# One more channel tile of a depthwise convolution moved from TensorE to ScalarE and GpSimd, in a hybrid decoder trunk

## The chip, the cores and the metric

The kernel runs on one core of a Trainium2 chip. A core has a matrix engine (TensorE, in the profile PE, with its weight loads as PEld), a vector engine (VectorE, DVE), a scalar engine (ScalarE, ACT), GpSimd (POOL) and a queue that issues DMAs (SyncE, SP). Each engine works through its own list of instructions in order, and semaphores tie the lists together. The metric is the device time of one launch in microseconds (us); lower is better.

## The reference

A trunk of two layers over 512 positions of 1024 channels, in float32. Layer 0 mixes tokens by a gated delta rule, layer 1 by a Conformer convolution module; each layer then attends to a memory of 256 positions and ends in an MLP. Only the Conformer module is touched:

```python
def conformer_conv(h, w_pw1, b_pw1, w_dw, b_dw, ln_g, ln_b, w_pw2, b_pw2):
    u = h @ w_pw1 + b_pw1
    u = u[..., :D_MODEL] * jax.nn.sigmoid(u[..., D_MODEL:])
    c = causal_depthwise_conv(u, w_dw) + b_dw
    c = jax.nn.silu(layer_norm(c, ln_g, ln_b))
    return c @ w_pw2 + b_pw2

# and in the trunk, for layer 1:
h = h + conformer_conv(rms_norm(h, cv_norm[j]), ...)
```

`causal_depthwise_conv` has a width of 31: each channel is convolved with its own 31 weights along the positions. The layer norm runs over the 1024 channels of a position.

## The kernel before

**Matrix products.** All of them run in float32 by splitting: a value is a high part (a cast, ACT) and a low part (value minus high part, DVE or POOL), and `mm3` (L227) multiplies high by high, high by low and low by high. Weights come in halves of 128x1024 from memory into `raw` (3 buffers); `wsplit` (L199) casts a half into `wh` (ACT, L207) and subtracts into `wl` (DVE or, for the halves of `pw1` and for every other half of K and V in layer 1, POOL; L70). `wh` and `wl` have 3 buffers each (`NW`), so the cast for half n waits until PE has done with half n-3.

**The Conformer stage** (`conformer`, L999) works on activations that lie channel by channel: 8 tiles m of 128 channels by 512 positions. The positions are kept in four phases (position modulo 4), so that a shift by d positions is a shift by d // 4 columns and a change of phase. `CONV_SEQ` (L1372) sets the order of PE's units: 16 units `("p", i)`, the two halves (value and gate) of the first pointwise product for each m, 24 products each; then 16 units `("k", i)`, the K and V products of the cross-attention that follows, which need nothing of the convolution and are there as work to lay beside it. `CONV_AFTER` (L1373) hangs other steps behind units. At the end of a tile's second half `pw_ev` (L1012) evicts both (`sg`, `pa` times the norm's `rb`, DVE), takes the sigmoid (ACT) and multiplies (DVE).

**The convolution has two forms.** For m = 0 to 3 (`NDVE` = 4) `dve_conv` (L1038) does it by taps: `x7` holds the four phases and the three shifted ones; the first tap is an ACT product into a PSUM tile `ca`, the 30 others are one DVE instruction each, `ca = x * w + ca` (L73); at the end ACT copies `ca` out (L1051). `turn` (L1059) then turns the tile back to positions by four PE transposes (`cvT`), adds it to the bias that lies in `Y` (DVE) and takes the statistics for the layer norm (`bn_stats`, DVE). For m = 4 to 7 `conv` (L1069) does it on PE: 16 small DMAs regroup the tile into `xg` (L1032), nine DMAs bring weights (`taps`, L991), and 72 products (64 of 128x128, L1078; 8 of 128x64, L1081) write `cv` already turned; DVE adds it to the bias in `Y` and takes statistics. `Y` (`cy`) is eight tiles, four of positions by two halves of channels, filled at the start with the bias by eight DMAs (L1006).

**The end of the stage.** `ln` (L1091) joins the statistics, takes the square root (ACT) and scales the eight `Y` tiles (DVE, L79). `ln_out` (L1106) turns a channel tile back (`lnT`, PE), applies silu (ACT, `la`) and splits the result (`lsh` ACT, `lsl` DVE). The second pointwise product, eight tiles of 24 PE products (`pw<-lsh`), needs all eight; its first result is evicted at `h<-pw`.

**Order.** The tile framework reorders instructions within each engine by its own priorities and writes out fixed lists; a tile whose buffer is taken waits for its release. What stands in an engine's list behind a waiting instruction waits with it.

Of the kernel before, what the change touches and what calls it, by code (L numbers as in the profile page):

```python
# [8 lines left out]
F32 = mybir.dt.float32  # L9
F32R = mybir.dt.float32r  # L10
AF = mybir.ActivationFunctionType
# [3 lines left out]
P = 128  # L15
NT = 512
NDVE = 4
KT = 8
# [3 lines left out]
_VECS = ["dn_norm", "cv_norm", "xa_norm0", "xa_norm1", "xa_mem0", "xa_mem1", "mlp_norm0", "mlp_norm1",  # L22
         "ln_g", "ln_b", "b_pw2"]
OFF = {n: 8 * i for i, n in enumerate(_VECS)}
# [5 lines left out]
OFF["w_tap"] = _o  # L30
_o += NDVE * 31
OFF["out_norm"] = _o
# [6 lines left out]
def tile_trunk(ctx, tc, xT, memT, prm_d, adt_d, bdw_d, tap_d, fin_d, w_ab, w_kq, w_v, w_z, w_dno, w_pw1, w_pw2,  # L39
# [951 lines left out]
    def taps(m):  # L991

        TAPS[m] = []
        for i in range(9):
            t = slot(s="tap")
            nc.sync.dma_start(out=t, in_=tap_d[m - NDVE, i])
            TAPS[m].append(t)

    def conformer(norm, hres, nxt):  # L999
# [4 lines left out]
        for y in Y:  # L1004
            for i in range(2):
                nc.sync.dma_start(out=y[i], in_=bdw_d[i * 512:(i + 1) * 512].partition_broadcast(P))  # L1006

# [4 lines left out]
        def pw_ev(m):  # L1012
# [4 lines left out]
            tt(dve, a, st.pop((m, 0)), norm.rb, ALU.mult)  # L1017
            if m < NDVE:
                x7 = fsp.tile([P, 1024], F32, tag="fs", name=nm("x7"))[:, 0:1008].rearrange("p (q t) -> p q t", q=7)
                pool.memset(x7[:, :, 0:10], 0.0)  # L1020
                stt(x7[:, 3:7, 8:136], c4(a), pc("b_pw1", m), c4(sg), ALU.add, ALU.mult)
                act.copy(x7[:, 0:3, 9:137], x7[:, 4:7, 8:136])
                todo.extend(dve_conv(m, x7))
                return
# [10 lines left out]

        todo, acc = [], {}

        def dve_conv(m, x7):  # L1038

            def tap(d):  # L1040
                w, u, e = pc("w_tap", m * 31 + 30 - d), d // 4, d % 4
                src = x7[:, 3 - e:7 - e, 8 - u:136 - u]
                if d == 0:
                    st["ca"] = psum("ca")
                    act.activation(c4(st["ca"]), src, AF.Copy, scale=w)  # L1045
                    return
                a = c4(st["ca"])
                stt(a, src, w, a, ALU.mult, ALU.add)
                if d == 30:
                    acc[m] = slot(s="ca")  # L1050
                    act.copy(acc[m], st.pop("ca"))  # L1051

            return [lambda d=d: tap(d) for d in range(31)]

        def taps_dve(us):
# [3 lines left out]
        def turn(m):  # L1059
# [4 lines left out]
            for r in range(4):  # L1064
                y = Y[r][m // 4][:, m % 4 * P:m % 4 * P + P]
                tt(dve, y, ps[:, r * P:(r + 1) * P], y, ALU.add)
                dve.bn_stats(out=bn[:, (r * 8 + m) * 6:(r * 8 + m) * 6 + 6], in_=y)
# [50 lines left out]
        for i, (kind, u) in enumerate(CONV_SEQ):  # L1118
            if kind == "p":
                m, hf = divmod(u, 2)  # L1120
                pw_mm(m, hf)
                if (m, hf) == (0, 0):
                    norm.stat()
                if (m, hf) == (1, 0):
                    norm.spread()
                    pw_ev(0)
                if hf == 1 and m > 0:
                    pw_ev(m)
            else:
# [179 lines left out]
    def finish(hid, cur):  # L1309
# [3 lines left out]
        for c, g in LAST:  # L1313
# [14 lines left out]
            if g == 0:  # L1328
# [69 lines left out]
def _taps(np, w):  # L1398
# [11 lines left out]
    e = np.concatenate([e[:, :, :, 0:8].reshape(128, 8, 128), e[:, :, :, 8].reshape(128, 8, 16)], axis=2)  # L1410
    e = e.reshape(4, 32, 8, 9, 16)[:, :, NDVE:]
    t = np.zeros((8 - NDVE, 9, 4, 32, 16, 32), w.dtype)
    for c in range(32):
        t[:, :, :, c, :, c] = e[:, c].transpose(1, 2, 0, 3)
    return t.reshape(8 - NDVE, 9, 128, 512)


def _layout(np, i):
# [3 lines left out]
    def vec(v):  # L1422
# [6 lines left out]
            i["xa_mem_norm"][1], i["mlp_norm"][0], i["mlp_norm"][1], i["cv_ln_g"][0],  # L1429
            i["cv_ln_b"][0], i["cv_b_pw2"][0], i["cv_b_pw1"][0]]  # L1430
    cols = [vec(v) for v in vecs]
    cols.append(i["dn_w_conv"][0].T.reshape(24, 128, 4).transpose(1, 0, 2).reshape(128, 96))
    cols.append(i["cv_w_dw"][0].T.reshape(8, 128, 31)[:NDVE].transpose(1, 0, 2).reshape(128, NDVE * 31))
    cols.append(i["dn_out_norm"][0].reshape(128, 1))
# [39 lines left out]
```

## Time and profile before

| What | Value |
|---|---|
| median of 3 runs | 1562.23 us (1561.81 to 1562.45) |
| the profiled execution | 1561.98 us, span 1560.3 us |
| mean granted TensorE clock | 0.991 |
| busy share of the span | PE 98%, DVE 58%, ACT 42%, POOL 12% |
| the Conformer's first product starts | 863.2 us into the span |
| its second pointwise product starts | 1041.2 us |
| first two results of that product evicted | 1047.90 and 1052.43 us |

All times of rows are from the start of the span. The profile shows a busy time, a start and what ended the idle time before an instruction; a group joins instructions of one line, engine and operation. PE's products overlap in the array, so the duration of one (0.39 us for 128x512) is longer than the step from one to the next (0.23 us), which counts for sums. DVE's instructions overlap a little too. A long product list such as `L229`/`L230`/`L231` is `mm3`.

### The profile page before, as it was taken

The numbers are of one execution on the slowest core, as the hardware profiler recorded it, in microseconds if no ns is written. First come the engines' busy times: TensorE is split into PE (matmuls) and PEld (weight loads), VectorE is DVE, ScalarE is ACT, GpSimd is POOL, SyncE is SP. The second block draws the span as 40 slices with busy tenths as digits, with TensorE's granted clock in tenths as the row PEclk, the third lists the DMA queues.
The fourth block names the chain that finished last, engine by engine and source line by source line (L and its number), as shares of the span: only waits on it lengthen the run. The fifth ranks groups of instructions, "written<-read, shape, count | busy, mean of one in ns | idle before, by whom it ended". The sixth has DMA issues, their size and how long they took to land.

```text
span 1560.3 us, 19403 instructions
## 1 busy us (share of the span) xinstructions
PE 1527.7 (98%) x7628; PEld 1285.7 (82%) x7628; DVE 901.2 (58%) x1373; ACT 655.0 (42%) x1018; POOL 187.0 (12%) x202
## 2 busy tenths in 40 slices
PE   9999996999999999999999999999999999999998
PEld 7888885988888888888888889978888888888886
DVE  6798887767555444343435499864545443444441
ACT  6847654554444433232314331264444432323332
POOL 1311212001112000000002441212112000000000
PEclk9999997999999999999999999999999999999999
DMA  5122121352212232222334625443203223332231
GB/s 181 55 87 68 63 78 46 107 189 69 91 58 78 88 101 99 95 95 95 99 100 155 200 87 166 161 141 95 80 29 108 95 96 100 101 96 95 95 108 54
DMA packets 51115, 156.17 MB, mean 100 GB/s; under 512 B 6608, under 2 KB 8912, under 8 KB 51024
## 3 DMA queue, kind: packets, MB, share of 16 engines
q1 hardware_dynamic: 51024, 154.93, 30.4%
q8 instruction: 60, 0.98, 0.3%
q14 instruction: 31, 0.25, 0.1%
HBM read 151.76 MB, written 2.10 MB: 99 GB/s over the span
## 4 chain that ended last, share of the span: by engine, by line
PE 90%; DVE 5%; issue 2%; ACT 1%; DMA 1%; SPq 1%; POOL 0%; DVEq 0%; POOLq 0%; ACTq 0%
PE up L229 7%; PE up L230 7%; PE up L231 7%; PE dn L229 7%; PE dn L231 7%; PE dn L230 7%; PE pw L229 3%; PE pw L231 3%; PE pw L230 3%; PE h L230 2%; PE h L229 2%; PE h L231 2%; PE q L229 2%; PE xo L230 2%; PE q L231 2%
## 5 line engine op out<-in xcount | busy, mean ns | idle before, releaser
L207 ACT CAST wh<-raw 128x1024 fp32r<-128x1024 f32 x248 | 260.4, 1051 | 673.9 <-PE dn L230 190.4
L70 DVE TENSOR_TENSOR wl<-raw,wh 128x1024 fp32r<-128x1024 f32 x224 | 275.6, 1231 | 97.3 <-ACT wh L207 95.9
L229 PE MATMUL up<-xh,wh 128*128 128x512 f32 x512 | 200.2, 391 | 0.0
L231 PE MATMUL up<-xh,wl 128*128 128x512 f32 x512 | 199.2, 389 | 0.0
L230 PE MATMUL up<-xl,wh 128*128 128x512 f32 x512 | 199.2, 389 | 0.0
L231 PE MATMUL dn<-uh,wl 128*128 128x512 f32 x448 | 174.3, 389 | 0.0
L229 PE MATMUL dn<-uh,wh 128*128 128x512 f32 x448 | 174.3, 389 | 0.0
L230 PE MATMUL dn<-ul,wh 128*128 128x512 f32 x448 | 174.3, 389 | 0.0
L70 DVE TENSOR_TENSOR h<-dn,h 128x512 f32<-128x512 f32 x56 | 41.8, 747 | 163.3 <-PE dn L231 163.3
L73 DVE SCALAR_TENSOR_TENSOR rl<-up,rb 128x512 f32<-128x512 f32 x64 | 44.2, 691 | 156.9 <-PE up L231 156.9
L229 PEld LDWEIGHTS up<-xh,wh 128*128 128x128 f32 x512 | 96.1, 188 | 20.3 <-issue 0.5
L231 PEld LDWEIGHTS up<-xh,wl 128*128 128x128 f32 x512 | 96.1, 188 | 20.2
L230 PEld LDWEIGHTS up<-xl,wh 128*128 128x128 f32 x512 | 96.1, 188 | 20.1 <-issue 0.5
L70 POOL TENSOR_TENSOR sq<-sq,sq 128x512 f32<-128x512 f32 x30 | 48.7, 1623 | 460.5 <-ACT sq L304 460.5
L231 PEld LDWEIGHTS dn<-uh,wl 128*128 128x128 f32 x448 | 84.1, 188 | 17.6
L230 PEld LDWEIGHTS dn<-ul,wh 128*128 128x128 f32 x448 | 84.1, 188 | 17.4
L229 PEld LDWEIGHTS dn<-uh,wh 128*128 128x128 f32 x448 | 84.1, 188 | 17.3
L73 DVE SCALAR_TENSOR_TENSOR ca<-x,prm,ca 128x512 f32<-128x512 f32 x120 | 88.0, 750 | 3.0 <-ACT ca L1045 1.2
L229 PE MATMUL h<-xh,wh 128*128 128x512 f32 x192 | 79.7, 415 | 1.7 <-ACT xh L297 1.7
L230 PE MATMUL h<-xl,wh 128*128 128x512 f32 x192 | 77.7, 405 | 0.6 <-DVE xl L73 0.6
L231 PE MATMUL h<-xh,wl 128*128 128x512 f32 x192 | 77.2, 402 | 0.0
L70 POOL TENSOR_TENSOR wl<-raw,wh 128x1024 fp32r<-128x1024 f32 x24 | 57.5, 2402 | 114.4 <-ACT wh L207 93.8
(336 smaller groups left out, 3024.6 us busy)
## 6 DMA issues: line engine op xcount, KB each, us to landing
raw<-w_up SPq DMA_DIRECT2D x64, 512.0 KB, 3.6
raw<-w_dn SPq DMA_DIRECT2D x64, 512.0 KB, 3.6
raw<-w_pw SPq DMA_DIRECT2D x24, 512.0 KB, 3.7
tap<-tap SPq DMA_DIRECT2D x36, 256.0 KB, 5.5
raw<-w_kq SPq DMA_DIRECT2D x16, 512.0 KB, 3.7
raw<-w_k SPq DMA_DIRECT2D x16, 512.0 KB, 3.8
raw<-w_vv SPq DMA_DIRECT2D x16, 512.0 KB, 4.2
raw<-w_q SPq DMA_DIRECT2D x16, 512.0 KB, 3.6
```

Of the source, the lines that this page charges most:

```text
L70: return e.tensor_tensor(out=o, in0=a, in1=b, op=op)
L73: dve.scalar_tensor_tensor(out=o, in0=a, scalar=s, in1=b, op0=op0, op1=op1)
L207: ins = [act.copy(h, raw)]
L229: pe.matmul(ps, wh, xh, start=first, stop=False)
L230: pe.matmul(ps, wh, xl, start=False, stop=False)
L231: pe.matmul(ps, wl, xh, start=False, stop=last)
```

## The change

It has six parts.

1. `NDVE` becomes `NTAP` = 5: the tiles m = 0 to 4 go by taps, m = 5 to 7 by PE. The weights for PE shrink to three tiles, and `pw_ev` and `taps` follow.
2. Tile m = 0 has a new form, `pool_conv`. Its input is laid into `xp` (four phases, no shifted copies). Tap 0 is an ACT product; each of the 30 others is an ACT product into a new tile `cvp` (one instruction where the shift keeps the phase, else two) and one POOL addition into `ca`. They are dealt out by `taps_pool`: two behind each `p` unit, one behind each `k` unit, three behind each `c` step. Tiles 1 to 4 take the DVE form.
3. The bias enters with the first tap (ACT, `AF.Identity` with a bias), and `turn` no longer adds: ACT copies each of the four transposed pieces to `Y`, and DVE takes the statistics from PSUM. Four of the eight bias DMAs fall away.
4. `CONV_AFTER` is new: the turns stand at their tiles' ends, the turn of tile 4 and the layer norm stand behind unit 27, and the eight `ln_out` behind units 29 to 31 (before: layer norm behind unit 23, `ln_out` behind units 26 to 31).
5. The norm's `spread` and the first `pw_ev` come one unit earlier.
6. The diagonal of that norm (`dg`) is made on DVE rather than POOL.

```diff
-NDVE = 4
+NTAP = 5
...
         for y in Y:
-            for i in range(2):
-                nc.sync.dma_start(out=y[i], in_=bdw_d[i * 512:(i + 1) * 512].partition_broadcast(P))
+            nc.sync.dma_start(out=y[1], in_=bdw_d[512:1024].partition_broadcast(P))
...
-            if m < NDVE:
+            if m == 0:
+                x4 = c4(wp.tile([P, 544], F32, tag="cv", name=nm("xp"), bufs=NCV))
+                pool.memset(x4[:, :, 0:8], 0.0)
+                stt(x4[:, :, 8:136], c4(a), pc("b_pw1", m), c4(sg), ALU.add, ALU.mult)
+                todo_p.extend(pool_conv(m, x4))
+                return
+            if m < NTAP:
...
+        def pool_conv(m, x4):
+            a = acc[m] = slot(s="ca")
+
+            def tap(d):
+                w, u, e = pc("w_tap", m * 31 + 30 - d), d // 4, d % 4
+                if d == 0:
+                    act.activation(c4(a), x4[:, :, 8:136], AF.Identity, scale=w, bias=pc("b_dw", m))
+                    return
+                b = slot(s="cvp")
+                act.activation(c4(b)[:, e:4], x4[:, 0:4 - e, 8 - u:136 - u], AF.Copy, scale=w)
+                if e:
+                    act.activation(c4(b)[:, 0:e], x4[:, 4 - e:4, 7 - u:135 - u], AF.Copy, scale=w)
+                tt(pool, a, a, b, ALU.add)
...
-                    act.activation(c4(st["ca"]), src, AF.Copy, scale=w)
+                    act.activation(c4(st["ca"]), src, AF.Identity, scale=w, bias=pc("b_dw", m))
...
+        def taps_pool(n):
+            for _ in range(min(len(todo_p), n)):
+                todo_p.pop(0)()
...
-                y = Y[r][m // 4][:, m % 4 * P:m % 4 * P + P]
-                tt(dve, y, ps[:, r * P:(r + 1) * P], y, ALU.add)
+                y = ps[:, r * P:(r + 1) * P]
+                act.copy(Y[r][m // 4][:, m % 4 * P:m % 4 * P + P], y)
                 dve.bn_stats(out=bn[:, (r * 8 + m) * 6:(r * 8 + m) * 6 + 6], in_=y)
...
-                if (m, hf) == (1, 0):
+                if (m, hf) == (0, 1):
                     norm.spread()
-                    pw_ev(0)
-                if hf == 1 and m > 0:
+                if hf == 1:
                     pw_ev(m)
             else:
                 kv_unit(1, u)
             taps_dve(5.4 if kind == "p" else 2.8)
+            taps_pool(2 if kind == "p" else 1)
             for what, m, *js in after.pop(i, ()):
...
+                taps_pool(3 if what == "c" else 0)
...
-    n3 = Norm("cv_norm", deng=pool)
-    h = mlp(0, n2, h, n3, lambda: (mem_gain(1, 0), mem_gain(1, 1), taps(NDVE)))
+    n3 = Norm("cv_norm")
+    h = mlp(0, n2, h, n3, lambda: (mem_gain(1, 0), mem_gain(1, 1), taps(NTAP)))
...
-CONV_AFTER = [(3, ("t", 5)), (11, ("d", 0)), (12, ("c", 4, 0, 1)), (13, ("c", 4, 2, 3)), (13, ("t", 6)),
-              (14, ("c", 5, 0, 1, 2, 3)), (14, ("t", 7)), (15, ("d", 1)), (16, ("c", 6, 0, 1, 2, 3)), (18, ("d", 2)),
-              (18, ("c", 7, 0, 1, 2, 3)), (23, ("d", 3)), (23, ("l", 0))]
-CONV_AFTER += [(_i, ("o", _m)) for _m, _i in enumerate((26, 27, 28, 29, 30, 30, 31, 31))]
+CONV_AFTER = [(3, ("t", 6)), (11, ("d", 1)), (13, ("c", 5, 0, 1, 2, 3)), (13, ("t", 7)), (15, ("c", 6, 0, 1, 2, 3)),
+              (16, ("d", 2)), (17, ("c", 7, 0, 1, 2, 3)), (19, ("d", 0)), (23, ("d", 3)), (27, ("d", 4)), (27, ("l", 0))]
+CONV_AFTER += [(_i, ("o", _m)) for _m, _i in enumerate((29, 29, 30, 30, 30, 31, 31, 31))]
```

The rest of the diff packs the weights and biases for the new split. In the instruction lists of the changed kernel, the four statistics and the four copies of a turn alternate strictly, each waiting for the other engine's last one.

More of the change, by code (lines that the diff above doesn't have):

```diff
@@ L22 @@
 _VECS = ["dn_norm", "cv_norm", "xa_norm0", "xa_norm1", "xa_mem0", "xa_mem1", "mlp_norm0", "mlp_norm1",
-         "ln_g", "ln_b", "b_pw2"]
+         "ln_g", "ln_b", "b_pw2", "b_dw"]
 OFF = {n: 8 * i for i, n in enumerate(_VECS)}
@@ L30 @@
 OFF["w_tap"] = _o
-_o += NDVE * 31
+_o += NTAP * 31
 OFF["out_norm"] = _o
@@ L995, in taps @@
             t = slot(s="tap")
-            nc.sync.dma_start(out=t, in_=tap_d[m - NDVE, i])
+            nc.sync.dma_start(out=t, in_=tap_d[m - NTAP, i])
             TAPS[m].append(t)
@@ L1034, in pw_ev @@
             xg[m] = x4
-        todo, acc = [], {}
+        todo, todo_p, acc = [], [], {}
+        def pool_conv(m, x4):
[10 more added lines that the diff above has]
+                tt(pool, a, a, b, ALU.add)
+            return [lambda d=d: tap(d) for d in range(31)]
         def dve_conv(m, x7):
@@ L1410, in _taps @@
     e = np.concatenate([e[:, :, :, 0:8].reshape(128, 8, 128), e[:, :, :, 8].reshape(128, 8, 16)], axis=2)
-    e = e.reshape(4, 32, 8, 9, 16)[:, :, NDVE:]
-    t = np.zeros((8 - NDVE, 9, 4, 32, 16, 32), w.dtype)
+    e = e.reshape(4, 32, 8, 9, 16)[:, :, NTAP:]
+    t = np.zeros((8 - NTAP, 9, 4, 32, 16, 32), w.dtype)
     for c in range(32):
         t[:, :, :, c, :, c] = e[:, c].transpose(1, 2, 0, 3)
-    return t.reshape(8 - NDVE, 9, 128, 512)
+    return t.reshape(8 - NTAP, 9, 128, 512)
 def _layout(np, i):
@@ L1429, in _layout @@
             i["xa_mem_norm"][1], i["mlp_norm"][0], i["mlp_norm"][1], i["cv_ln_g"][0],
-            i["cv_ln_b"][0], i["cv_b_pw2"][0], i["cv_b_pw1"][0]]
+            i["cv_ln_b"][0], i["cv_b_pw2"][0], i["cv_b_dw"][0], i["cv_b_pw1"][0]]
     cols = [vec(v) for v in vecs]
     cols.append(i["dn_w_conv"][0].T.reshape(24, 128, 4).transpose(1, 0, 2).reshape(128, 96))
-    cols.append(i["cv_w_dw"][0].T.reshape(8, 128, 31)[:NDVE].transpose(1, 0, 2).reshape(128, NDVE * 31))
+    cols.append(i["cv_w_dw"][0].T.reshape(8, 128, 31)[:NTAP].transpose(1, 0, 2).reshape(128, NTAP * 31))
     cols.append(i["dn_out_norm"][0].reshape(128, 1))
```

## The prediction

> **What bounds it now.** I read the page first, then the stage's stretches, the chain of waits, and the instructions of DVE and POOL in order of time.
>
> ```profile
> PE 1527.7 (98%) x7628; PEld 1285.7 (82%) x7628; DVE 901.2 (58%) x1373; ACT 655.0 (42%) x1018; POOL 187.0 (12%) x202
> ```
> ```profile
> 900.00:920.00 20.00, 20.00 (x90) 16.57 (x89) 19.58 (x29) 7.18 (x10) 8.39 (x5) 1.00 0.32 105
> ...
> 1020.00:1040.00 20.00, 17.85 (x82) 14.34 (x83) 13.06 (x18) 14.13 (x19) 3.07 (x2) 0.91 0.44 141
> ```
>
> PE is the bound overall: only work taken off PE, or a wait of PE, moves the end. The stretches (columns: length, then busy time of PE, PEld, DVE, ACT, POOL, then clock) show that in the Conformer DVE is as full as PE (19.6 of 20 us), while ACT and POOL have room. PE loses time only at the end of the stage, where the chain leaves it:
>
> ```profile
> 1015.94 0.76 DVE mv L1094 x3
> ...
> 1017.90 1.01 DVE cy L79 x2
> 1018.91 1.97 issue
> ...
> 1023.30 0.48 PE lnT L1109
> 1023.77 0.43 PE V L262
> 1028.27 0.23 PE V L262
> ```
>
> Statistics, square root and scaling of `Y` lead to the first `lnT`; PE waited for it and then ran its V products at 0.43 us instead of 0.23, with the clock at 0.91 over that stretch.
>
> **The change on PE.** Tile 4's products go:
>
> ```profile
> 955.37 1.78 PE cv L1078 x16
> ...
> 963.36 0.28 PE pw L229
> ```
> ```profile
> 930.47 0.44 PE cvT L1062 x4
> 869.90 0.23 PE pw L230
> 868.77 0.79 PE ssq L315 x8
> 880.60 0.86 PE rb L325 x2
> ```
> ```profile
> 980.20 0.28 PE L230 MATMUL K<-ml,wh 128*128 128x256 f32 x1
> 985.72 0.28 PE L231 MATMUL K<-mh,wl 128*128 128x256 f32 x1
> ```
>
> A tile is 963.36 - 955.37 = 8.0 us; one more turn costs 0.44: PE has 7.55 us less. That much is the gain if nobody makes PE wait. PE's work up to the turn of tile 4, behind unit 27: 16 units of 24 products at 0.2335 = 89.7; `ssq` and `rb` 1.65; three conv tiles 24.0; eight K units, 192 products at 0.12 (46 steps between the two K rows) = 23.0; four turns 1.8; four V units, 48 products at 0.234 = 11.2. Sum 151.4, from 863.2: PE could be there at 1014.6.
>
> **The change on DVE.** It keeps four tiles of 30 taps, so its end is the question. Rows of before:
>
> ```profile
> 882.12 0.69 DVE L70 TENSOR_TENSOR sg<-pw,rb 128x512 f32<-128x512 f32 x1 [12.05 <-ACT rb L327]
> 886.08 7.09 DVE L73 SCALAR_TENSOR_TENSOR ca<-x,prm,ca 128x512 f32<-128x512 f32 x9 [1.17 <-ACT ca L1045]
> 939.02 0.48 DVE L70 TENSOR_TENSOR cy<-cvT,cy 128x128 f32<-128x128 f32 x2
> 976.20 1.22 DVE L70 TENSOR_TENSOR wl<-raw,wh 128x1024 fp32r<-128x1024 f32 x1
> 997.10 0.29 DVE L70 TENSOR_TENSOR cy<-cv,cy 128x128 f32<-128x128 f32 x1 [2.21 <-PE cv L1081]
> 980.23 0.49 DVE L70 TENSOR_TENSOR cy<-cv,cy 128x128 f32<-128x128 f32 x2 [1.36 <-PE cv L1081]
> 1004.36 1.53 DVE L73 SCALAR_TENSOR_TENSOR ca<-x,prm,ca 128x512 f32<-128x512 f32 x2
> ```
>
> First tap to last: 886.1 to 1005.9, 119.8 us. By the new instruction list, this stretch loses one tile's eviction (the first DVE tile is m = 1: two of 0.60 and one of 0.65, -1.85), 16 small additions and statistics net (56 become 40, at 0.20 step: -3.2) and the waits of 2.21 and 1.36 (-3.6); it gains three weight splits that stood later (1.14 each, +3.4) and four K evictions (0.60 each, +2.4): 117.0 us. It begins later: tile 1's second half ends at 863.2 + 4 x 5.6 + 1.65 = 887.3, and from the first eviction to the first tap it took 4.0 (882.1 to 886.1) with a table load that goes, but now with a cast of 1.05 ahead of the sigmoid: 892.0. So the taps would end at 1009.0 if POOL left DVE alone. It doesn't:
>
> ```profile
> 858.88 2.40 POOL L70 TENSOR_TENSOR wl<-raw,wh 128x1024 fp32r<-128x1024 f32 x1 [1.34 <-ACT wh L207]
> ```
> ```profile
> 859.80 2.02 DVE L73 SCALAR_TENSOR_TENSOR xl<-h,prm,xh 128x512 fp32r<-128x512 f32 x1 [0.79 <-ACT xh L297]
> ```
> ```profile
> L73 DVE SCALAR_TENSOR_TENSOR x<-pa,prm,sg x4: 746/748/753, 884.2 to 916.2; 128x512 f32<-128x512 f32 x4
> ```
> ```profile
> L70 POOL TENSOR_TENSOR cva<-cva,cvq 128x512 f32<-128x512 f32 x12 | 15.5, 1292 | 60.7 <-ACT cvq L459 58.6 <-issue 2.0
> ```
>
> `xl`, two tensors from SBUF, took 2.02 us and ended at 861.82, just 0.54 after POOL's split (861.28): it had been held up. The taps, with one tensor in PSUM, keep their step beside POOL. POOL's addition is 1.29 (`cva`). Now POOL gets 30 of them, 38.8 us, in the stretch where its splits take 2.40 per unit: in two units (11.2 us) two splits and four additions, 10.0 us, so it keeps up, but is busy nine tenths. DVE's two-input instructions in the tap stretch are seven products of value and gate, about six weight splits that meet POOL, and three `Kl`: 16. A random arrival waits (2 x 2.40² / 2 + 4 x 1.29² / 2) / 11.2 = 0.81 us beside `pw1`; I take 0.81 x 7 = 5.7, and 0.3 x 9 = 2.8 beside K and V, where POOL has about one split per two units of 5.8 us: L = 8.5 us. The bounds of L: 0 (none meets) to 38 (each waits a whole split of 2.40). I take the mean, since the starts of both hang on PE's unit ends and fall within a few us of each other.
>
> Against it stands the row of the four value-gate products (`x`): 0.746 to 0.753, never held up, with POOL busy 8.4 of 20 us. The Trainium skill, page "SBUF — State Buffer", section "Who interferes with whom", has the rule: a VectorE instruction with two SBUF inputs and a GpSimd instruction that reads SBUF exclude each other, each for the other's whole length, while one with at most one SBUF input does not contend. By the `x` row alone L would be 2.8 and the kernel at the first rival's 1555; by the rule it is the 8.5 used here. `xl`, the same operation with two SBUF tensors, sides with the rule.
>
> Taps end at 1009.0 + 8.5 = 1017.5. ACT copies the tile out (about 0.6, an estimate from half the `Vh` pair below), PE turns it (0.44): C = 1018.8, and PE has waited about 3.7 us since 1014.6.
>
> **ACT, SP.**
>
> ```profile
> 992.27 0.59 SPq L1032
> 992.90 1.84 DMA xg<-glu
> ```
>
> ACT's added 30 taps cost at most the 0.78 of a row below each, 23 us over 130; it has 12 us free in 20 (7.18 busy above), so nothing is charged. If ACT fell behind, POOL's sums would be late first, but tile 0 is turned 25 us ahead of tile 4. SP issues 29 DMAs fewer (9 weights, 4 biases, 16 regroupings); tile 7's regrouping starts after its product on DVE near 970 and lands, at 16 x 0.59 + 1.84, before PE needs the last quarter near 983. `dg` on DVE costs one instruction of about 0.7 in an idle stretch (12.05 us before the first eviction), and `spread` one unit earlier moves 0.86 of PE without changing it.
>
> **From C to the second product.**
>
> ```profile
> 1020.53 1.28 ACT L1111 ACT_TABLE_LOAD   x1
> 1037.98 0.78 ACT L1111 ACTIVATE la<-lnT,prm 128x512 f32<-128x512 f32 x1
> 1039.31 0.78 ACT L1111 ACTIVATE la<-lnT,prm 128x512 f32<-128x512 f32 x1
> 1040.65 1.05 ACT L207 CAST wh<-raw 128x1024 fp32r<-128x1024 f32 x1
> 1041.60 1.26 ACT L817 ACTIVATE Vh<-V,mtok 128x512 fp32r<-128x512 f32 x2
> 1052.43 0.75 DVE L73 SCALAR_TENSOR_TENSOR h<-pw,prm,h 128x512 f32<-128x512 f32 x1 [1.78 <-PE pw L231]
> ```
>
> After the last turn ACT's copies and DVE's statistics alternate; between the second and third ACT must cast the half for unit 31, which waits for the end of unit 28 (C + 2.8), so the statistics are joined at about C + 6.5. A cast (1.05), the table load (1.28), square root and reciprocal (on four columns, estimated at 0.5 together): C + 9. Seven scalings at 0.5 and the turn: `lnT` of tile 0 is complete at C + 12.5. PE has 40 V products until then (9.4) and waits some 1 us. Silu 0.78; the next cast waits for V's last product: C + 15. Then eight tiles at 1.33 (1037.98 to 1039.31) and `Vh` 1.26 on ACT: C + 26.9, one low part and the last six products 1.5: the first two results are complete at C + 28.4 = 1047.2. Before, the second was evicted at 1052.43: a gain of about 5.1 us, and behind it nothing changes. No row shows the copy of a 128x128 piece by ACT or the handshake; between 0.2 and 0.7 us each for four, I took 0.25 and keep 2 us either way.
>
> **Sum.** 7.55 off PE; of what PE lost in 1020 to 1040 (20 - 17.85 = 2.15 idle, and 0.09 of 20 by the clock, 1.8) 4.0 comes free; 3.7 go to the wait before the turn, and from C PE's own work is 11.2 of V, 3.5 of `lnT` and 11.2 of the product, 25.9, so that 28.4 holds 2.5 of waits: 7.55 + 4.0 - 3.7 - 2.5 = 5.3, which agrees with 5.1 by dates. The profiled execution took 1561.98, of which 1560.3 is the span, and the median is 1562.23: I say 1557.
>
> **Rivals.** First, DVE is not held up (L under 6): then PE's own list and the cast for unit 30 ahead of the copy set C at 1016.9, a gain of 7.0, up to 9 with shorter handshakes: 1553 to 1555. For it: the `x` row of 0.75; against it: POOL was then idle more than half the time. Second, no change that can be told: PE's wait of 3.7 us before the last turn halves the clock as in the rows at 1023.77, at 0.43 for 0.23 some 1.7 us over a window, unit 28 ends later and with it the cast in the middle of the handshakes, about 3 us in all, and with the 2 us of the handshakes the gain is near 1: 1561. The Trainium skill, "TensorE: Matmul & The Clock Gate", Part 1, puts the drop to half after an idle window of about 3.4 us, which the 3.7 would just fill; the rows here show the half rate at 1023.77 and not the window. Third, slower: L. Each us of it beyond 8.5 is a us of C; from L = 13.6, 0.85 for each of the 16, the kernel is no longer faster, and at 1.2 each (19) it takes 1567.5; at the bound 1587. For it: POOL nine tenths busy, and DVE without slack; against it: two of three POOL instructions there are the short additions, and an arrival sees half of one.
>
> **Chances.** Forecast 0.42 (gain 3.1 to 7: 1555 to 1559); DVE not held up 0.22; no change 0.23; slower 0.13. A measurement tells 0.2%, 3.1 us: faster 0.64, same 0.23, slower 0.13. The range that leaves out the far ends of the first and the third rival is 1553 to 1564.
>
> **What would show it.** Right: conv products 192 and 24 instead of 256 and 32; POOL's `ca` sums at 1.3 us, longer when they meet DVE; the value-gate products on DVE above 0.75 in the mean; the last tap near 1017; a PE wait before the last `cvT` of 2 to 5 us; the second `h<-pw` near 1047. Wrong: PE waits for POOL's `wl` in the `pw` units (then POOL is the bound), or for `xg`; the last tap beyond 1023; V products at 0.43 for longer than one window; or a stage as long as before with waits among the `lnT`.

## The result, and the profile after

The changed kernel takes 1555.64 us (median of 6 runs, 1555.13 to 1558.07), the kernel before 1561.96 us (6 runs, 1560.85 to 1562.45). The ratio is 0.9963 with a 95% interval of 0.9952 to 0.9975: the median is 6.3 us lower, and the interval of the ratio is a gain of 3.9 to 7.5 us. The profiled execution took 1555.59 us (before: 1561.98), so that the profiles can be compared as they stand.

The first part of the page, the busy time of each engine over the whole span:

```profile
PE 1519.2 (98%) x7560; PEld 1277.0 (82%) x7560; DVE 902.6 (58%) x1354; ACT 682.6 (44%) x1092; POOL 226.4 (15%) x231
```

PE is busy 8.5 us less (fewer products, and none of them at half clock any more), POOL 39.4 us more (30 sums of 1.29 us are 38.7). Next the stretches of the changed kernel in the columns of the prediction (length, busy PE, PEld, DVE, ACT, POOL, clock, DMA share, GB/s):

```profile
940.00:960.00 20.00, 17.72 (x113) 15.61 (x112) 18.83 (x33) 9.13 (x18) 14.99 (x11) 1.00 0.33 102
...
1020.00:1040.00 20.00, 17.82 (x92) 14.12 (x91) 15.89 (x29) 15.73 (x22) 0.00 (x0) 1.00 0.39 130
```

PE now loses time in three places, where before it was one: 2.3 us near 943, 1.8 near 1016, 2.2 near 1033. The clock stays at 1.00; before it fell to 0.91 in the last of these stretches. What PE waited for in the changed kernel, from 840 to 1100 us (sum, times, longest):

```profile
PE cv L1103 <- DMA xg<-glu: 2.3, 3, 1.6
PE cvT L1087 <- ACT ca L1072: 1.8, 1, 1.8
PE lnT L1134 <- ACT la L1136: 1.5, 1, 1.5
PE pw L229 <- ACT la L1136: 0.7, 1, 0.7
```

And the whole stage in one row per kernel (840 to 1090 us, the same columns). The kernel before:

```profile
840.00:1090.00 250.00, 246.38 (x1336) 212.12 (x1336) 184.43 (x291) 94.51 (x121) 75.90 (x37) 0.99 0.43 140
```

The changed kernel:

```profile
840.00:1090.00 250.00, 243.74 (x1300) 208.57 (x1299) 187.75 (x275) 124.76 (x198) 115.04 (x66) 1.00 0.40 127
```

PE was idle for 3.62 us before (250 less 246.38) and is for 6.26 us now. So the account is: 7.55 us of work off PE, 1.8 us of half clock gone, 2.64 us more idle, together 6.7; the profiled executions differ by 6.4. The last eviction of the second pointwise product starts 6.3 us earlier, at 1078.8 for 1085.1, and behind that nothing differs. The question for the experiments is what paid: the tile, or something that came with it.

### The profile page after: what moved, and what is told of

It reads as the page before. It is cut to its first block, busy times and chain, and to the rows that moved or that the text cites. A ratio compares the mean times of both kernels' runs of the same rounds, so it can differ in the third digit from the quotient of the medians.

```text
span 1553.8 us, 19346 instructions
## 1 busy us (share of the span) xinstructions
PE 1519.2 (98%) x7560; PEld 1277.0 (82%) x7560; DVE 902.6 (58%) x1354; ACT 682.6 (44%) x1092; POOL 226.4 (15%) x231
## 4 chain that ended last, share of the span: by engine, by line
PE 88%; DVE 7%; issue 2%; ACT 1%; SPq 1%; DMA 0%; POOL 0%; DVEq 0%; ACTq 0%; POOLq 0%
PE up L229 7%; PE up L230 7%; PE up L231 7%; PE dn L229 7%; PE dn L231 7%; PE dn L230 7%; PE h L230 2%; PE h L229 2%; DVE ca L73 2%; PE h L231 2%; PE q L229 2%; PE xo L230 2%; PE q L231 2%; PE xo L229 2%; PE q L230 2%
```

## The experiments

Every run is compared with the kernel before on its own chip. PE idle is 250 less its busy time from 840 to 1090 us, in one profile of each run.

| Run | Median, us | Before, us | Ratio (95%) | PE idle, us |
|---|---|---|---|---|
| kernel before | 1561.96 | | | 3.62 |
| changed kernel | 1555.64 | 1561.96 | 0.9963 (0.9952 to 0.9975) | 6.26 |
| e1, turn, spread and `dg`, tile 4 on PE | 1556.91 | 1562.25 | 0.9965 (0.9953 to 0.9978) | 0.60 |
| e2, additions back on DVE | 1558.31 | 1562.25 | 0.9977 (0.9968 to 0.9987) | 6.78 |
| e3, no POOL sums | 1554.43 | 1562.25 | 0.9952 (0.9940 to 0.9965) | 4.27 |
| e4, spread late | 1556.04 | 1562.25 | 0.9959 (0.9947 to 0.9972) | 6.21 |
| e5, before, `lnT` one unit later | 1558.92 | 1562.45 | 0.9979 (0.9970 to 0.9987) | 1.63 |
| e6, tile 5's products later | 1554.98 | 1562.45 | 0.9957 (0.9944 to 0.9971) | 5.12 |
| e7, ten taps off DVE | 1557.02 | 1562.45 | 0.9963 (0.9951 to 0.9976) | 6.41 |
| e8, taps dealt out faster | 1562.21 | 1561.93 | 1.0000 (0.9991 to 1.0009) | 10.34 |
| e9, e8 and the turn earlier | 1562.60 | 1561.93 | 1.0005 (0.9997 to 1.0014) | 11.09 |
| e10, the changed kernel again | 1556.83 | 1562.09 | 0.9962 (0.9950 to 0.9975) | 6.11 |
| e11, the turn alone | 1557.79 | 1562.09 | 0.9974 (0.9963 to 0.9984) | 1.11 |
| e12, products and scalings reordered | 1558.03 | 1562.09 | 0.9972 (0.9961 to 0.9983) | 6.23 |

### Is it the tile? e1, e5 and e11

The first run takes the tile out again, with the order behind the units as before, and leaves the turn, the bias, `spread` and `dg`. Against the changed kernel:

```diff
-NTAP = 5
+NTAP = 4
...
-            if m == 0:
-                x4 = c4(wp.tile([P, 544], F32, tag="cv", name=nm("xp"), bufs=NCV))
...
-                todo_p.extend(pool_conv(m, x4))
-                return
...
-CONV_AFTER = [(3, ("t", 6)), (11, ("d", 1)), (13, ("c", 5, 0, 1, 2, 3)), ...
+CONV_AFTER = [(3, ("t", 5)), (11, ("d", 0)), (12, ("c", 4, 0, 1)), ...
```

> The kernel before with the bias in the first tap, the turn by ScalarE copies, spread and first eviction one unit earlier, and dg on DVE; the fifth tile stays on PE and the order behind the units is that of before. Theory (the gain is the PE time of the fifth tile): PE has the same products as before and got to the last turn behind the taps' end anyway (taps ended at 1005.9, PE could be there at about 1011), so that earlier taps release nobody; 1561.5, within 2 us of before. Rival (the gain comes from these parts, which lift DVE and shorten what follows the last turn): the two losses of PE at the end of the stage, 2.15 us idle and 1.8 us of clock, go, and the time falls to 1558 or below.

It takes 1556.91 us, 5.3 less than before, with all of tile 4's products back on PE: the rival, and a little more. The stage of this run in one row:

```profile
840.00:1090.00 250.00, 249.40 (x1366) 215.49 (x1365) 190.49 (x280) 100.68 (x140) 76.44 (x36) 1.00 0.43 137
```

PE is idle for 0.60 us. That is 3.0 us less than before, and the 1.8 us of half clock are gone too: 4.8 of the 5.3. Where from, PE's own rows say. The kernel before, around the first `lnT` (start, duration, engine, line, operation; in brackets the wait ahead):

```profile
1019.22 0.27 PE L1109 MATMUL lnT<-ident,cy 128*128 128x128 f32 x1
1021.47 0.33 PE L1109 MATMUL lnT<-ident,cy 128*128 128x128 f32 x1 [1.98 <-DVE cy L79]
1022.38 0.33 PE L1109 MATMUL lnT<-ident,cy 128*128 128x128 f32 x1 [0.58 <-DVE cy L79]
1022.47 0.48 PE L260 MATMUL V<-wh,mh 128*128 128x512 f32 x1
...
1023.42 0.78 PE L262 MATMUL V<-wh,ml 128*128 128x512 f32 x1
```

The same place in the run e1:

```profile
1020.19 0.30 PE L1128 MATMUL lnT<-ident,cy 128*128 128x128 f32 x1 [0.60 <-DVE cy L79]
1020.25 0.48 PE L261 MATMUL V<-wl,mh 128*128 128x512 f32 x1
...
1021.03 0.32 PE L1128 MATMUL lnT<-ident,cy 128*128 128x128 f32 x1
```

Each of the four transposes of a channel tile needs another scaled `Y` (`cy`). Before, three of them stand in a row, with V products free to run behind them, and PE waits twice for a scaling; soon after, it runs at half clock (0.78 for 0.48). In e1 the tile framework has put V products between the transposes.

The longer of the two waits, 1.98 us, has a cause of its own. The scalings on DVE (min, median, max in ns) and a weight split on POOL in the kernel before:

```profile
L79 DVE TENSOR_SCALAR cy<-cy,mv,lrs x8: 534/536/2597, 1017.9 to 1023.2; 128x512 f32<-128x512 f32 x8
```
```profile
1018.24 2.43 POOL L70 TENSOR_TENSOR wl<-raw,wh 128x1024 fp32r<-128x1024 f32 x1 [3.83 <-ACT wh L207]
```

The second scaling started at 1018.4, took 2.60 us instead of 0.54 and ended at 1021.0, just behind that split (1020.67); the third, which PE's second transpose needs, could only follow. The same meeting, a scaling that starts within 0.3 us behind a split and takes 2.63 us, stands in e5, e7 and e9, so it is read here as DVE waiting for POOL. In e1 and e11 the split starts 1.8 us ahead of the first scaling, and the longest scaling takes 0.90. So two things differ there from the kernel before: the transposes stand apart, and no scaling is held for 2 us. If the place of the transposes is enough, moving them in the kernel before should do nearly the same.

```diff
-CONV_AFTER += [(_i, ("o", _m)) for _m, _i in enumerate((26, 27, 28, 29, 30, 30, 31, 31))]
+CONV_AFTER += [(_i, ("o", _m)) for _m, _i in enumerate((27, 28, 29, 29, 30, 30, 31, 31))]
```

> The kernel before with one edit: the first four transposes of the layer norm's output stand behind units 27, 28, 29, 29 instead of 26, 27, 28, 29. No tile, no bias, no turn is touched. Theory (the run with the turn alone gained 5.3 us because its four lnT of the first tile no longer stand in one block that waits for four scalings, 2.6 us, and then runs on at half clock, 1.8 us): the block comes 2.8 us later, the scalings are done, neither loss is left, and the time is 1557 to 1558.5. Rival (the gain of that run is DVE's and ScalarE's changed turn itself): within 1 us of before, 1561 to 1562.5.

1558.92 us: three numbers changed in a list, 3.5 us. The block now stands one V unit later; its first three transposes run without a wait, and the fourth waits (e5, PE):

```profile
1024.56 0.33 PE L1109 MATMUL lnT<-ident,cy 128*128 128x128 f32 x1 [0.58 <-DVE cy L79]
```

The time lies 0.4 us above the range that the theory gave, but far from the rival. A scaling is held here too (2.63 us), but PE comes to the transposes only when it is over. So the place of the transposes is worth 3.5 us by itself. That leaves the question which part of the change loosens the block. In PE's written-out list it is the turn (part 3): with it alone the four transposes of the first tile stand apart. (With `spread` alone, part 5, they stand as before in that list; no run shows that kernel.) Against the kernel before, the run e11 has part 3 only:

```diff
-                    act.activation(c4(st["ca"]), src, AF.Copy, scale=w)
+                    act.activation(c4(st["ca"]), src, AF.Identity, scale=w, bias=pc("b_dw", m))
...
-                y = Y[r][m // 4][:, m % 4 * P:m % 4 * P + P]
-                tt(dve, y, ps[:, r * P:(r + 1) * P], y, ALU.add)
+                y = ps[:, r * P:(r + 1) * P]
+                act.copy(Y[r][m // 4][:, m % 4 * P:m % 4 * P + P], y)
```

> The kernel before with the third part alone: the bias in the first tap, and the turn by ScalarE copies with the statistics from PSUM; spread, first eviction, dg and the order behind the units stay as before. In the written-out order of PE the first tile's four lnT then stand apart among V products, as in the run with parts 3, 5 and 6; with part 5 alone they stand in one block as before. Theory (the block is what cost the kernel before its idle time and its half clock): 1557 (1556.5 to 1558). Rival (the earlier start of the taps by part 5 is what gained): 1560.5 or more.

1557.79 us, 4.3 less than before, PE idle 1.11 us. So the turn alone has 4.3 us, with `spread` and `dg` 5.3 (their intervals overlap), and the whole change 6.3 on one chip and 5.3 on another (e10). Whether the turn gains by setting the transposes apart or by moving the split away from the scalings, these runs don't tell; both go with it. The changed kernel's ratio cannot be told from that of e1 (0.9963 and 0.9962 beside 0.9965). Moving the tile itself, with its order, is by the medians worth between nothing and some 1 us, and the intervals leave room for some 3 us either way, although it takes 7.55 us of work off PE: PE's idle time goes from 0.60 to 6.26 us, 5.7 of the 7.55.

> The changed kernel itself, unaltered, beside the next two on one chip: 1555.6 (1555 to 1556.5).

The repeat came out at 1556.83 (1554.24 to 1557.45), 0.3 us above the expected range, ratio 0.9962; that is how far one chip and another differ.

### Who makes PE wait now? e2, e3 and e4

The run e2 undoes the turn in the changed kernel:

```diff
-                y = ps[:, r * P:(r + 1) * P]
-                act.copy(Y[r][m // 4][:, m % 4 * P:m % 4 * P + P], y)
+                y = Y[r][m // 4][:, m % 4 * P:m % 4 * P + P]
+                tt(dve, y, ps[:, r * P:(r + 1) * P], y, ALU.add)
```

> The changed kernel with the bias back in Y by DMA and DVE's additions back in the turn instead of ScalarE's copies. Theory (DVE sets the last turn): 20 additions of about 0.24 us each come back to DVE, 4.8 us, of which 1 to 2 are regained because the handshake of ScalarE and DVE falls away; the last turn 3 us later, 1558.5 (1557.5 to 1560). Rival (the handshake costs as much as the additions, or DVE has slack): 1555 to 1556.5.

1558.31, inside the theory's range, and the last `cvT` starts at 1019.3 instead of 1017.3. But PE does not wait for the turn itself; it waits newly for these:

```profile
PE K L231 <- DVE wl L70: 1.7, 1, 1.7
...
PE V L261 <- POOL wl L70: 0.9, 1, 0.9
```

DVE's added work shows in its weight splits, which PE needs in the K units. PE's idle time is only 0.5 us more than in the changed kernel (6.78). What sets the two profiled executions apart (1557.38 and 1555.59) is mostly the clock: it is at 0.91 from 1000 to 1020, some 1.8 us, right behind these two waits. The time agreed with the theory; its mechanism is not what the profile shows.

The run e3 leaves out POOL's sums (tile 0 then has its first tap only):

```diff
-                tt(pool, a, a, b, ALU.add)
```

> The changed kernel without GpSimd's 30 additions; ScalarE's products for them stay, so tile 0 has its first tap only (this leaves out part of the convolution). Theory (GpSimd's reads hold up DVE's two-input instructions): the value-gate products are all at 0.75 us, DVE's last tap ends about 4 us earlier, near 1012, PE arrives at the last turn near 1014 and doesn't wait there, and its wait ahead of the conv products of tile 5 shrinks; 1553 (1552 to 1554). Rival (the wait ahead of the last turn is lockstep of PE, casts and weight splits, and the conv wait is the order of the DMAs): 1555 to 1556.

1554.43 us, between the ranges of theory and rival: 7.8 less than before, against 6.3, though the intervals overlap; the profile has 2.0 us less PE idle. The value-gate products of the PE tiles in the changed kernel (min, median, max in ns):

```profile
L73 DVE SCALAR_TENSOR_TENSOR glu<-pa,prm,sg x3: 1350/1803/1934, 934.8 to 967.6; 128x512 f32<-128x512 f32 x3
```

and in e3, with PE's waits:

```profile
L73 DVE SCALAR_TENSOR_TENSOR glu<-pa,prm,sg x3: 743/744/747, 936.9 to 966.4; 128x512 f32<-128x512 f32 x3
```
```profile
PE cvT L1086 <- ACT ca L1071: 1.8, 1, 1.8
...
PE cv L1102 <- DMA xg<-glu: 0.3, 1, 0.3
```

The three products go back to 0.74, and of the wait for tile 5's regrouping 0.3 of 2.3 is left. So POOL's sums reach PE through `glu`, whose DMAs start late; the theory has that half right. The sums do it mostly by shifting POOL's own splits: of the three held products the first two (934.76 and 947.29) began while a split ran (from 933.60 and 946.32), only the third while a sum did (from 967.08). The other half fails: the last tap ends 1.6 us earlier (1014.7), not 4, and PE still waits 1.8 us ahead of the last turn, because it came there earlier too. (The products of the DVE tiles do not all come free: POOL's splits still hold two of them, at 1.75 and 1.94.)

The run e4 puts `spread` and the first eviction back by one unit:

```diff
-                if (m, hf) == (0, 1):
+                if (m, hf) == (1, 0):
                     norm.spread()
-                if hf == 1:
+                    pw_ev(0)
+                if hf == 1 and m > 0:
```

> The changed kernel with spread and the first eviction back behind unit 2 (one unit, 5.6 us, later). Theory (DVE's taps set the last turn, without slack): the first tap, and with it the last, is 4 to 5 us later, of which PE's 1.8 us wait there is no cover; 1559.5 to 1560.5. Rival (PE's own list sets the turn and DVE has slack): not above 1556.5.

1556.04: nothing. The expectation was wrong in its own reasoning. The first eviction is now that of tile 0, which POOL sums; DVE's first tap belongs to tile 1 and starts at 892.68, as in the changed kernel (892.20). The run shows only that POOL's tile has slack: its last sum starts at 972.0 instead of 968.4, and nobody waits for it.

### Can the waits be had back? e6, e7, e8, e9 and e12

Four waits of PE were known by then, and the next runs each move one cause. In e6 tile 5's products stand one unit later:

```diff
-(13, ("c", 5, 0, 1, 2, 3)), (13, ("t", 7)),
+(14, ("c", 5, 0, 1, 2, 3)), (14, ("t", 7)),
```

> The changed kernel with the PE products of tile 5 one unit later (behind unit 14 instead of 13), so that its regrouping has landed. Theory (the 2.3 us wait for it is a loss of PE, and the last turn follows PE by the cast for unit 30 and the copy, since DVE's last two taps stand behind a weight split that itself waits for PE): everything behind comes 2 us earlier, 1553.5 (1553 to 1554.3). Rival (DVE is full and its taps end at 1016 whatever PE does): PE waits that much longer ahead of the last turn, 1555 to 1556.

1554.98: 7.5 less than before, against 6.3, inside the changed kernel's interval; the time lies above the theory's range, just below the rival's. PE's waits in e6:

```profile
PE cvT L1087 <- ACT ca L1072: 1.8, 1, 1.8
...
PE cv L1103 <- DVE ca L73: 1.1, 1, 1.1
```

The 2.3 us are gone, 1.1 of them are back at the next tile's products, and the other three waits (1.8, 1.5, 0.7) are the same to a tenth. In the changed kernel, e3, e4, e6 and e10 the wait ahead of the last turn is 1.8 us each time, whenever PE comes. The chain of waits of the changed kernel shows why:

```profile
1012.49 1.06 ACT wh L207
...
1013.58 1.23 DVE wl L70
1014.81 0.68 DVE ca L73
...
1015.51 0.77 DVE ca L73
...
1016.94 0.66 PE cvT L1087 x4
```

The last two taps stand in DVE's list behind a weight split, which needs a cast, which waits for PE to leave the unit three before. And ACT has its own reason to be late, in its list just ahead of the copy:

```profile
1015.21 1.04 ACT L207 CAST wh<-raw 128x1024 fp32r<-128x1024 f32 x1 [1.66 <-PE V L262]
1016.30 0.58 ACT L1072 COPY ca<-ca 128x512 f32<-128x512 f32 x1
```

That cast waits for PE's unit 27, the one right ahead of the turn, and ends at 1016.25 when the taps end at 1016.26. Both ways the wait counts from PE's own units, so it moves with PE. This is read from the lists and fits the equal waits; no run breaks the loop by itself.

The run e7 takes the last ten taps of tile 4 off DVE, keeps tile 5's products behind unit 14, and puts the turn two units earlier (the `lnT` behind units 28, 28, 29, 29, 30, 30, 31, 31):

```diff
+                if d >= n:
+                    b = slot(s="ca" if d == n else "cvp")
+                    if d == n:
+                        acc[m] = b
+                    act.activation(c4(b), src, AF.Copy, scale=w)
+                    if d > n:
+                        tt(pool, acc[m], acc[m], b, ALU.add)
+                    return
...
+                        tt(dve, acc[m], st.pop("ca"), acc[m], ALU.add)
...
-... (23, ("d", 3)), (27, ("d", 4)), (27, ("l", 0))]
+... (22, ("d", 3)), (25, ("d", 4)), (25, ("l", 0))]
```

> The changed kernel with the last ten taps of tile 4 as ScalarE products and GpSimd sums (one DVE addition joins the two parts), tile 5's products one unit later, the turn of tile 3 behind unit 22, the turn of tile 4 and the layer norm behind unit 25, and the lnT behind units 28, 28, 29, 29, 30, 30, 31, 31. Theory (PE's 6.3 us of waits in this stage are all waits for a work order that comes late, and with DVE 6 us lighter the last turn can stand two units earlier): PE waits at most 1 us in the stage, 1550 (1549.3 to 1551.5). Rival (the chain from the last turn to the first lnT is bound by the handshakes and by ScalarE whatever stands ahead): 1553 to 1555.

1557.02, no better than the changed kernel, and PE as idle (6.41): 2.0 us ahead of tile 6's products, 1.8 among the `lnT`, behind a scaling that a split of POOL held (2.63 us for 0.54), and 2.5 for two weight splits of DVE. DVE's two-input instructions in e7:

```profile
994.33 2.75 DVE L71 TENSOR_TENSOR Kl<-kf,Kh 128x512 fp32r<-128x512 f32 x1
...
1000.25 2.49 DVE L71 TENSOR_TENSOR wl<-raw,wh 128x1024 fp32r<-128x1024 f32 x1
...
1006.85 3.40 DVE L71 TENSOR_TENSOR wl<-raw,wh 128x1024 fp32r<-128x1024 f32 x1
```

beside POOL's at the last of them:

```profile
1006.78 2.40 POOL L71 TENSOR_TENSOR wl<-raw,wh 128x1024 fp32r<-128x1024 f32 x1 [5.12 <-DVE ca L71]
```

`wl` took 3.40 us instead of 1.22 and ended 1.07 us behind a POOL split that had started 0.07 us ahead of it: a whole POOL instruction waited out. Over 980 to 1013 DVE's `wl` and `Kl` took 6.9 us more than their 1.22 and 0.68, against 1.2 in the changed kernel's tap stretch: as much as the ten taps had freed. Two of the three rows are waits of PE (1.4 for the last `wl`, 1.1 for the one before). Neither theory nor rival had this.

The runs e8 and e9 leave the work where it is and let the taps come earlier in DVE's list (e9 also puts the last turn behind unit 25):

```diff
-TAP_RATE = 1.1
+TAP_RATE = 1.25
...
-            for r in range(4):
-                for y in Y[r]:
+            for i in range(2):
+                for r in range(4):
+                    y = Y[r][i]
...
-(13, ("c", 5, 0, 1, 2, 3)), ... (17, ("c", 7, 0, 1, 2, 3)),
+(14, ("c", 5, 0, 1, 2, 3)), ... (18, ("c", 7, 0, 1, 2, 3)),
```

> The changed kernel with the taps dealt out faster (TAP_RATE 1.25 for 1.1: 7 behind a pw1 unit for 6, 4 behind a K or V unit for 3), tile 5's products behind unit 14 and tile 7's behind unit 18, and the layer norm scaling the first channel halves of all four Y first. The turn of tile 4 stays behind unit 27. DVE's list then has the last tap ahead of the K units' evictions, and ScalarE's copy stands ahead of the cast for unit 30. Theory (the 1.8 us ahead of the last turn, the same in four runs, is the order of cast and copy, not DVE's work): that wait and the waits for regrouping go, the tail's 2.2 us shrinks to about 1.5; 1552 (1551 to 1553). Rival (DVE is full: what the taps overtake, evictions and weight splits, comes late, and PE waits there instead): 1555 or more.

> As the run with the taps dealt out faster, and the turn of tile 4 and the layer norm behind unit 25 instead of 27, the lnT behind units 28, 28, 29, 29, 30, 30, 31, 31. Theory: the layer norm's chain (about 9 us from the last turn to the first scalings) lies under V units, so that PE's tail waits go too; 1550.5 (1549.5 to 1552). Rival (DVE cannot have the taps done by then, as with ten taps off it): PE waits 2 to 5 us ahead of the last turn or for weight splits; 1554 to 1557.

1562.21 and 1562.60: all of the gain is lost, as the rivals said and worse. Tile 7's eviction on DVE in the changed kernel, then the same and the tile's products on PE in e8:

```profile
965.04 0.68 DVE L70 TENSOR_TENSOR sg<-pw,rb 128x512 f32<-128x512 f32 x1
```
```profile
984.68 0.69 DVE L70 TENSOR_TENSOR sg<-pw,rb 128x512 f32<-128x512 f32 x1
```
```profile
991.82 3.75 PE L1103 MATMUL cv<-tap,xg 128*128 128x128 f32 x16 [7.18 <-DMA xg<-glu]
```

One tap more per unit pushes DVE's evictions of the late tiles back (by 19.6 us for tile 7) until the regrouping of tile 7 makes PE wait 7.18 us, and the products then start at half clock (3.75 for 2.0). DVE has no time to spare in the pointwise units; what one thing overtakes there comes late.

The last run keeps the deal of the taps and moves only PE's products and the order of the scalings (the last two edits of e8):

> The changed kernel with order alone altered, and the taps dealt out as in it: tile 5's PE products behind unit 14 (for 13), tile 7's behind unit 18 (for 17), and the layer norm scaling the first channel halves of all four Y first. Theory (DVE's list must not be pushed; the waits for regrouping go by moving the products alone, and la and lsh of the first tile come ahead of the cast that waits for V's last product): against the changed kernel 2.3 us of waits for tile 5, and 0.6 of the tail go, 1553.2 (1552.5 to 1554). Rival (as with the taps dealt out faster or moved to GpSimd, DVE is full and PE waits elsewhere): 1554.8 to 1556.

1558.03, above the ranges of both. The waits for regrouping are gone, as expected, and PE is at the last turn about 1.7 us earlier than in the changed kernel. There it waits 4.6 us. The chain of waits:

```profile
1004.43 2.42 POOL wl L70
...
1006.86 3.98 DMA raw<-w_vv
...
1010.95 1.05 ACT wh L207
...
1012.19 0.31 DVE bn L1092
...
1014.70 1.22 DVE wl L70
```

A `raw` buffer comes free when POOL has split it; then the load of the next half takes 4 us; ACT's cast waits for it, behind the cast stands a copy of the turn before, and DVE's statistics wait for the copy, with the taps behind them. Why this loop bites here and not in the changed kernel the runs don't show. PE's idle time is in sum that of the changed kernel (6.23 and 6.26); what e12 loses is clock, 0.94 from 1000 to 1020 and 0.93 from 1020 to 1040, together some 2.6 us. No run has beaten the changed kernel by more than its interval.

## Why the prediction was right or wrong

The time, 1557, lies 1.4 us above the result, and inside the range of the forecast case, 1555 to 1559. By its condition it is rather the first rival that came: DVE was held for 4.1 us, under that rival's 6. Its time, 1553 to 1555, was missed by the wait for regrouping, which no case had. The forecast's account is right for some terms and wrong for others that happened to pay for each other.

**PE's work.** 192 and 24 conv products, as said. By its own work PE would have been at the last turn at 1012.8, not 1014.6, mainly because the step of a product there is 0.227 us and not 0.2335 (2.5 us on 384 of them): it came at 1015.1 after 2.3 us of waiting.

**The wait for regrouping.** Under "ACT, SP" only tile 7 was followed to its DMAs, and a wait for `xg` was named as a sign of being wrong. It came, at tile 5. The lists show what was overlooked: before, each tile's products stood three units behind its second half (tile 5's 14 behind 11), now two (13 behind 11). e3 shows that without POOL's lock on `glu` two units would nearly do, e6 that three do. This 2.3 us is missing in the sum.

**DVE's taps.** First tap 892.2 (forecast 892.0), last tap's end 1016.26 (1017.5). The 117.0 us without POOL hold; L does not. These are the instructions of the tap stretch that were held, and the places where DVE waited:

```profile
934.76 1.80 DVE L73 SCALAR_TENSOR_TENSOR glu<-pa,prm,sg 128x512 f32<-128x512 f32 x1
947.29 1.93 DVE L73 SCALAR_TENSOR_TENSOR glu<-pa,prm,sg 128x512 f32<-128x512 f32 x1
959.28 1.23 DVE L70 TENSOR_TENSOR wl<-raw,wh 128x1024 fp32r<-128x1024 f32 x1 [0.92 <-ACT wh L207]
967.55 1.35 DVE L73 SCALAR_TENSOR_TENSOR glu<-pa,prm,sg 128x512 f32<-128x512 f32 x1
986.07 0.29 DVE L70 TENSOR_TENSOR cy<-cv,cy 128x128 f32<-128x128 f32 x1 [0.58 <-PE cv L1106]
990.00 1.23 DVE L70 TENSOR_TENSOR wl<-raw,wh 128x1024 fp32r<-128x1024 f32 x1 [0.30 <-ACT wh L207]
993.99 1.89 DVE L70 TENSOR_TENSOR Kl<-kf,Kh 128x512 fp32r<-128x512 f32 x1
1006.46 0.30 DVE L1092 BATCH_NORM_STATS2 bn<-cvT 128x6 f32<-128x128 f32 x1 [1.24 <-ACT cy L1091]
```

The locks are 1.05 + 1.18 + 0.60 + 1.21 and 0.04 elsewhere, 4.1 us instead of 8.5; the waits are 3.0 us and were not counted. 117.0 + 4.1 + 3.0 is the 124.1 measured from 892.2 to 1016.3. The step that failed is the mean of a random arrival, in both its parts. Of the seven products beside `pw1`, three met nothing, the PE tiles' three lost 0.6 to 1.2 each, and tile 1's lost 1.0 ahead of the first tap: 3.9 in all for 5.7. The nine instructions beside K and V lost 1.2 for 2.8. The rule behind it holds: the Trainium skill, "SBUF — State Buffer", "Who interferes with whom", lets a VectorE instruction with two SBUF inputs wait for the whole of a GpSimd instruction that reads SBUF, and e7's 3.40 us row shows just that, while the row `x` of 0.75 was no protection.

**The last turn.** C = 1017.6 (1018.8), with a wait of 1.8 us (3.7; the text gave 2 to 5 as the sign). Neither DVE's taps alone nor PE's own work alone sets it: the first rival's words, the cast for unit 30 ahead of the copy, describe the place, and the weight split ahead of the last taps is its equal. The same 1.8 us in five runs speaks against DVE alone setting C at this load; what one more microsecond of L would cost, no run shows cleanly.

**From C to the second product.** Statistics joined at C + 6.4 (forecast 6.5), reciprocal C + 8.4 (9). The 48 products of the first two results end at 1046.2, C + 28.6 (28.4), but the second is evicted only at C + 31.7, since DVE had two weight splits ahead of it; PE waited 2.2 us there (2.5). The estimate of the handshakes was good: a copy took 0.26 us (0.25).

**"4.0 comes free".** It was 5.4: all 3.6 us of PE's idle time before and 1.8 of clock. Here the account was wrong in what matters most. The text let this come free along with the tile and never asked what set it free. It shows the 1.97 us in its chain, as `issue` at 1018.91, and puts them down to statistics, square root and scaling; they are one scaling behind a split of POOL. e5 gets 3.5 us by moving the transposes of three channel tiles one unit on, e11 4.3 by the turn alone, e1 5.3 without the tile. The 7.55 us, the first and largest term of the sum, bought 0 to 1 us by the medians.

**The rivals.** The half clock of the second rival did not come at a wait of 1.8 us; in e12 it came at 4.6, and again after 0.94 and 0.67, in e2 after 0.95 and 1.72. The third rival, DVE without slack, stayed under its point here, but e8 and e9 show how near it was. The sum thus agreed with the result because 7.55 + 5.4 - 2.3 - 1.8 - 2.2 = 6.65 differs little from 7.55 + 4.0 - 3.7 - 2.5 = 5.35. That the number came so near is in good part luck: the missing 2.3 and the waits and the free part that were mis-sized happen to cancel, and most of the gain did not need the tile.

## What to carry to other kernels

Where PE is the bound but waits at one place, first try to move the waiting instruction in PE's list: three numbers gave more than half of what this change gave. Work taken off the bounding engine and given to engines that are full beside it comes back as waits; compare the idle time of the bound, not the work. And follow each engine's list at the place of the wait: a wait that keeps its length when the engine comes earlier may be a loop through its own earlier units, and then making the suspected engine faster won't shorten it. Look also at the longest instruction of a group and not only at its mean: one scaling of 2.60 us among eight of 0.54 was the largest wait of the kernel before.

## What the runs showed of the hardware

**The half clock does not follow the length of the gap alone.** In the kernel before, PE ran no products but three transposes from 1019.2 to 1022.5, 3.3 us, and from 1023.4, about 1 us after they had begun again, its products ran at half clock. In the changed kernel it was without products from 1031.0 to 1034.9, 3.9 us with twelve transposes, and the clock stayed at 1.00. In e12 a stretch of the same kind from 1033.6 to 1036.9 (3.3 us, twelve transposes, waits of 0.94 and 0.67; another 2.0 us of transposes alone lay before it, from 1029.1) was followed by half clock:

```profile
1036.87 0.50 PE L229 MATMUL pw<-lsh,wh 128*128 128x512 f32 x1 [0.67 <-ACT la L1137]
...
1038.28 0.63 PE L231 MATMUL pw<-lsh,wl 128*128 128x512 f32 x1
```

The Trainium skill, "TensorE: Matmul & The Clock Gate", Part 1, describes an activity window of about 3.4 us that runs freely, so that the phase decides, and its Part 4 says that transposes do not count as busy in the same way. A phase would let one stretch drop and a longer one not. But 3.3 us are short of a full window, so this alone does not account for the drops, and no run here shows the window itself. No transposes are needed either: in e2 PE ran one V product between 1001.3 and 1004.4, with waits of 0.95 and 1.72 around it, and was at half clock from 1005.0 to 1008.4. The stretch of the changed kernel kept full clock in all five profiles that have it (waits of 1.5 and 0.7, also in e3, e4, e6 and e10), so nothing here shows that its outcome varies. Over whole executions the clock does vary a little: those of the changed kernel have a mean granted clock of 0.991 to 0.993 (e10 included), and the longest (1558.07 us) has the lowest, the shortest (1554.24) the highest; 0.001 of the span is about 1.6 us.

**The lock of DVE by POOL depends on the meeting, not on the load.** With 30 sums added it cost DVE 4.1 us in the tap stretch; without them (e3) 2.6 us are left, lost to POOL's splits alone. In e7 with 39 sums it is 6.9 us in 33 us, all of it on weight splits and `Kl`, which had lost 1.2 in the changed kernel. And one meeting at the wrong place is enough: in the kernel before, a single scaling held for 2.1 us made PE wait 1.98, and a scaling has one whole tensor as its input, not two. It can be measured after the fact; a mean over random arrivals (8.5) was off by a factor of two.
